# One RWKV step builds its keys in their final tile first and multiplies the decays in afterwards

## The chip, the cores and the metric

One Trainium2 chip, one NeuronCore. The metric is the device time of one execution in microseconds. Below, PE is TensorE, DVE is VectorE, ACT is ScalarE, POOL is GpSimd and SP is the engine that issues most transfers.

## What is computed

The reference is a two-layer backbone. In each layer one input projection feeds a Conformer convolution branch and a bidirectional RWKV-7 branch side by side; an output projection and a SwiGLU feed-forward part follow. 512 latent tokens and 256 context tokens go through the same weights. The part that matters here prepares, for each direction d, the operands of the recurrence:

```python
decay = jnp.exp(-DECAY_SCALE * jax.nn.sigmoid(decay_b0[d] + jnp.tanh(w_lo) @ decay_up[d]))
a = jax.nn.sigmoid(iclr_b0[d] + a_lo @ iclr_up[d])
k_d = k * (1.0 + (a - 1.0) * k_a)
...
s = (s * w_t[:, :, None, :] + sa[..., None] * b_t[:, :, None, :]     # b_t = kk * a
     + v_t[..., None] * k_t[:, :, None, :])
```

The kernel runs the recurrence in chunks of 64 tokens. Within a chunk the running product P of the decays is folded into the operands: `kk` and `r` are multiplied by P, and the two keys, `k_d` and `kk * a`, are divided by P. Products of these scaled operands (Gram matrices) then replace the token-by-token loop.

## The kernel before

**Stages.** Each layer has a mixing stage (projection, convolution and recurrence woven together) and a feed-forward stage. Mixing is cut into 12 blocks: 4 pairs of heads times 3 groups, each of 4 chunks per direction.

**What a block passes through.** `prep(b)` makes the operands of both directions. `grams(b)` multiplies them on PE (the tile names `KR` and `bk` in its matmuls: `pw<-KR,bk`), DVE masks the products into `G`. `base(b)` inverts small triangles by way of DRAM (`G`, `d0`, `Dt`, `XT`, `dimg`, `Tm`) and `levels` extends the inverses. `tokens(b)` transposes `bk` on PE (`pw<-cst,bk`, L938). `chain(b, s)` is the recurrence itself: a round of small steps PE, ACT, PE, ACT/DVE, PE, DVE (`Z`, `UV`, `S`), where each round needs the state `S` of the one before; POOL computes `Q`, the decayed state.

**What sets the order.** On PE the order is written by hand: a plan with first slots and widths weaves these generators between the matmuls of the projection (`pd<-h,wh` and `pd<-h,wl`), 16 slots to a block. In the pass for block b, `prep(b+2)` starts at slot 2 and ends at slot 6, and `z_part(b+2)`, which holds `grams`, stands from slot 9. On DVE, ACT, POOL and SP a scheduler sets the order by priority and readiness when the program is built. DVE also has the taps of the 31-tap convolution to do (`acc<-z,cw,acc`, about 0.9 us each in the first layer).

**`prep` and its tiles.** For each direction two matmuls with `lr` give the raw decays and the raw rates in one PSUM bank `pz`. The scratch `tmp` has three parts: `lx` (the logarithm of the decays, summed by the scan in L867), `px` (its exponential, P) and `qx` (1/P). The scratch `tw` holds tanh of the raw rates. `tmp`, `tw` and `bk` have one buffer each, so direction 1 can start to write `tmp` only when every reader of direction 0's `tmp` is done, and a block's `bk` can be written only when the block before no longer needs it. Within a direction: ACT does a tanh into `lx`, a tanh into `tw` and a scaling; DVE scans; ACT takes two exponentials; then ACT writes the key's factor `e` over `lx` (L233, `tmp<-tw,der`), which has to wait until the exponentials have read `lx`. DVE multiplies `e` by k (`tmp<-tmp,k`), makes (tw+1)*kk in place (`tw<-tw,kk`), makes the one or two parts of `KR`, and ends with the two products with 1/P into `bk` (`bk<-tmp` and `bk<-tw,tmp`). ACT copies a half of `bk` (`bk<-bk`) into a third place and a column of P into `pc`.

Helpers record many operations under one line: `act` L233, `stt` L236, `tt` L239, `ts` L242, `mm` L245.

Of the kernel before, what the change touches and what calls it, by code (L numbers as in the profile page):

```python
# [14 lines left out]
AF = mybir.ActivationFunctionType  # L15
# [166 lines left out]
def net(ctx: ExitStack, tc: tile.TileContext, I, out):  # L182
# [13 lines left out]
    def nm(s):  # L196
        uid[0] += 1
        return f"{s}_{uid[0]}"
# [29 lines left out]
    def bank(tag="w"):  # L228
        pool = {"d": pd, "w": pw, "c": pc_}[tag]
        return pool.tile([128, 512], F32, tag=tag, name=nm("p" + tag))  # L230

    def act(out, in_, func=AF.Copy, **k):
        return A.activation(out=out, in_=in_, func=func, **k)  # L233

    def stt(out, in0, scalar, in1, op0, op1, **k):
        V.scalar_tensor_tensor(out=out, in0=in0, scalar=scalar, in1=in1, op0=op0, op1=op1, **k)  # L236

    def tt(out, a, b, op):
        return V.tensor_tensor(out=out, in0=a, in1=b, op=op)  # L239
# [4 lines left out]
    def mm(out, lhsT, rhs, start=True, stop=True):  # L244
        PE.matmul(out=out, lhsT=lhsT, rhs=rhs, start=start, stop=stop)  # L245
# [15 lines left out]
    MUL, ADD, SUB = ALU.mult, ALU.add, ALU.subtract  # L261
# [354 lines left out]
    for l in range(DEPTH):  # L616
# [9 lines left out]
        der = lp.tile([128, 36], F32, tag="der", name=nm("der"))  # L626
# [201 lines left out]
        def nat(d, gi, cc):  # L828
            if d == 0:
                return (8, 0, 4)[gi] + cc  # L830
            return (11, 7, 3)[gi] - cc

        def dcols(ap, d, gi):

            if d == 0:
                c0 = C * nat(0, gi, 0)
                return ap[:, c0:c0 + 256].rearrange("p (c t) -> p c t", t=64)
            c0 = C * nat(1, gi, 3)
            return ap[:, c0:c0 + 256][:, ::-1].rearrange("p (c t) -> p c t", t=64)
# [3 lines left out]
        def prep(b):  # L843
            p, gi = divmod(b, 3)
            P = PS[p]
            emit = not (last and gi == 0)
            wl = u["wl"]
            KR = s2.tile([128, 2, 4, 2, 64], F32, tag="KR", name=nm("KR"), bufs=3)
            bk = s1.tile([128, 2, 4, 3, 64], F32, tag="bk", name=nm("bk"))
            pc = s2.tile([128, 2, 4], F32, tag="pc", name=nm("pc"), bufs=4)  # L850
            fl = lambda q: q.rearrange("p c t -> p (c t)")
            for d in range(2):
                pz = bank()
                lo = C * (nat(0, gi, 0) if d == 0 else nat(1, gi, 3))
                for j in range(2):
                    mm(pz[:, 256 * j:256 * j + 256], P["lr"][:, d, j, :], wl[:, lo:lo + 256])
                tmp = s1.tile([128, 3, 4, 65], F32, tag="tmp", name=nm("tmp"))
                tw = s1.tile([128, 4, 64], F32, tag="tw", name=nm("tw"))
                rv = lambda q: q if d == 0 else q[:, ::-1]

                lx, px, qx = (tmp[:, j] for j in range(3))
                G.memset(lx[:, :, 0:1], 0.0)  # L862
                act(lx[:, :, 1:65], rv(pz[:, 0:256]).rearrange("p (c t) -> p c t", t=64), AF.Tanh, scale=0.5,
                    bias=der[:, 4 * d + p:4 * d + p + 1])
                act(fl(tw), rv(pz[:, 256:512]), AF.Tanh, scale=0.5, bias=der[:, 8 + 4 * d + p:9 + 4 * d + p])
                act(lx[:, :, 1:65], lx[:, :, 1:65], AF.Copy, scale=-DS / 2, bias=-DS / 2)
                V.tensor_tensor_scan(out=fl(lx), data0=fl(one65), data1=fl(lx), initial=0.0, op0=MUL, op1=ADD)  # L867
                act(fl(px), fl(lx), AF.Exp)
                act(fl(qx), fl(lx), AF.Exp, scale=-1.0)

                e = lx[:, :, 0:64]
                act(e, tw, AF.Identity, scale=der[:, 16 + p:17 + p], bias=der[:, 20 + p:21 + p])
                tt(e, e, dcols(P["k"], d, gi), MUL)
                stt(tw, tw, 1.0, dcols(P["kk"], d, gi), ADD, MUL)
                tt(KR[:, d, :, 0, :], dcols(P["kk"], d, gi), px[:, :, 0:64], MUL)
                if emit:
                    tt(KR[:, d, :, 1, :], dcols(u[f"r{p}"], d, gi), px[:, :, 1:65], MUL)
                tt(bk[:, d, :, 0, :], e, qx[:, :, 1:65], MUL)
                stt(bk[:, d, :, 1, :], tw, 0.5, qx[:, :, 1:65], MUL, MUL)
                act(bk[64:128, d, :, 2, :], bk[64:128, d, :, 0, :])  # L880
                act(pc[:, d, :], px[:, :, 64])
                yield

            vr = s1.tile([128, 4, 64], F32, tag="vr", name=nm("vr"))
            act(vr, dcols(u[f"v{p}"], 1, gi))
            BS[b] = dict(KR=KR, bk=bk, vr=vr, pc=pc, emit=emit, G={}, tT={}, UV={}, T={})
            yield
# [347 lines left out]
        def nsteps(names):  # L1235

            return [-(-c // PCOL) for c in np.cumsum([work(n) for n in names])]
# [29 lines left out]
        with tc.manual_schedule(engines={mybir.EngineType.PE}):  # L1267
            for name, ps in zip(FIRST, pf):
                finish(name, ps)
            e = nsteps(FILL0[l])  # L1270
            B8 = 24 * T / PCOL
            start = {"pair_prep": (pair_prep(0), 3), "prep0": (prep(0), 3), "z0": (z_part(0), 3), "tok00": (tokens(0, 0), 2),
                     "tok01": (tokens(0, 1), 2), "prep1": (prep(1), 3), "z1": (z_part(1), 3), "t0": (t_part(0, 0), 4),
                     "tok10": (tokens(1, 0), 2)}
            weave(*((e[0] + d * B8, w * B8, *reversed(start[n])) for n, (d, w) in plan["prologue"].items()), (0, e[-1], e[-1], proj))
# [5 lines left out]
            for b in range(12):  # L1281
                p, gi = divmod(b, 3)
# [29 lines left out]
                if b + 2 < 12:  # L1312
                    lane("prep", prep(b + 2), 3)
                    lane("z", z_part(b + 2), 3)
                    lane("tok0", tokens(b + 2, 0), 2)
# [176 lines left out]
```

## Time and profile before

| what | value |
|---|---|
| median of 3 runs | 2211.42 us (2211.22 to 2214.58) |
| the profiled execution | 2219.2 us, its span 2217.3 us |
| first layer's mixing stage | about 68 to 620 us of the span |
| second layer's mixing stage | about 1340 to 1800 us |
| PE, DVE, ACT busy over the span | 2064.7, 1451.0, 945.2 us |
| mean granted PE clock | 0.97 of full speed |

Of the profiled execution's 2219.2 us, 1.9 us lie around its span. It was 7.8 us above the median of the runs that were not profiled. All rows of the profile come from this one execution. In a timeline row the first number is the start in microseconds, the second the time to the end of the last of the merged instructions; square brackets give the engine's idle time just before and what ended it.

### The profile page before, as it was taken

Reading aid. Unit: us, or ns where it says so; the run is one execution under the profiler, and the core shown is the slowest. Engines: PE = TensorE matmul, PEld = TensorE weight load, DVE = VectorE, ACT = ScalarE, POOL = GpSimd, SP = SyncE. Lnnn points to the kernel's source line nnn. Section 1 sums busy time; section 2 is a strip of 40 time slices with the busy share of each in tenths; the row PEclk is TensorE's granted clock in tenths of the full one; section 3 lists DMA queues with packets and bytes.
Section 4 is the critical chain, followed back from the end, with each engine's and each line's share of the span. In section 5 each row is a group of like instructions: output and inputs, shape, how many; then the busy total and the mean of one; then the engine's idle time right before and its main releaser. Section 6 shows DMA issues by size and latency. Waiting matters only on the chain.

```text
span 2217.3 us, 44128 instructions
## 1 busy us (share of the span) xinstructions
PE 2064.7 (93%) x17578; PEld 1663.5 (75%) x17578; DVE 1451.0 (65%) x3286; ACT 945.2 (43%) x2186; POOL 203.1 (9%) x528
## 2 busy tenths in 40 slices
PE   5999999998899999999999999999999889999997
PEld 4777777776687888878888876667676568888886
DVE  5578888877758565565653766777877765433446
ACT  4454645555425211212112545665657444222223
POOL 0102131211010000000000000122212010000000
PEclk9999999999899999999999999998999999999998
DMA  7232232243552343343432412121213442333233
GB/s 289 68 82 64 79 85 77 61 109 106 160 192 75 125 142 122 113 146 114 125 113 87 141 41 76 32 62 37 76 35 92 131 148 77 95 98 102 86 98 121
DMA packets 197804, 226.32 MB, mean 102 GB/s; under 512 B 110560, under 2 KB 140000, under 8 KB 197472
## 3 DMA queue, kind: packets, MB, share of 16 engines
q1 hardware_dynamic: 196448, 221.42, 33.2%
q8 instruction: 138, 2.26, 0.4%
q10 hardware_dynamic: 1152, 2.10, 0.2%
q14 instruction: 66, 0.54, 0.1%
HBM read 196.62 MB, written 26.85 MB: 101 GB/s over the span
## 4 chain that ended last, share of the span: by engine, by line
PE 61%; DVE 13%; ACT 10%; issue 7%; DMA 6%; POOL 3%; SPq 0%; POOLq 0%; DVEq 0%; ACTq 0%
PE pd L245 30%; PE pw L245 24%; PE pc L245 5%; DMA at<-in_adaT 4%; ACT tmp L233 2%; DVE wl L239 2%; DVE junk L236 2%; ACT UV L233 1%; DVE acc L236 1%; PE pw L950 1%; PE pw L419 1%; DVE xtmp L239 1%; DVE acc L239 1%; PE pw L938 1%; POOL rq L406 1%
## 5 line engine op out<-in xcount | busy, mean ns | idle before, releaser
L245 PE MATMUL pd<-h,wh 128*128 128x512 f32 (+3 forms) x2496 | 687.3, 365 | 3.6 <-ACT h L233 3.0
L233 ACT ACTIVATE wh<-raw 128x1024 fp32r<-128x1024 f32 (+2 forms) x234 | 220.8, 943 | 675.0 <-PE pw L245 258.7
L245 PEld LDWEIGHTS pd<-h,wh 128*128 128x128 f32 (+1 forms) x2496 | 425.2, 190 | 74.9 <-ACT h L233 3.7
L245 PE MATMUL pd<-h,wl 128*128 128x512 f32 (+3 forms) x1248 | 426.4, 364 | 2.8 <-DVE wl L239 2.8
L239 DVE TENSOR_TENSOR wl<-raw,wh 128x1024 fp32r<-128x1024 f32 (+2 forms) x234 | 253.8, 1085 | 131.4 <-ACT wh L233 130.4
L245 PE MATMUL pw<-h,wh 128*128 128x512 f32 (+1 forms) x1264 | 317.4, 350 | 4.5 <-DVE x L236 2.9
L245 PEld LDWEIGHTS pd<-h,wl 128*128 128x128 f32 (+1 forms) x1248 | 224.1, 190 | 38.7 <-DVE wl L239 4.2
L245 PEld LDWEIGHTS pw<-h,wh 128*128 128x128 f32 x1264 | 211.2, 190 | 40.1 <-DVE x L236 4.8
L236 DVE SCALAR_TENSOR_TENSOR junk<-at,cr 128x1024 bf16<-128x1024 f32 x112 | 136.9, 1223 | 114.2 <-DMA at<-in_adaT 113.2
L236 DVE SCALAR_TENSOR_TENSOR acc<-z,cw,acc 128x497 f32<-128x497 f32 (+20 forms) x216 | 192.9, 893 | 4.3 <-ACT acc L233 2.8
L245 PE MATMUL pw<-h,wl 128*128 128x512 f32 (+1 forms) x632 | 193.0, 351 | 0.0
L245 PE MATMUL pd<-mid,wh 128*128 128x512 f32 (+1 forms) x568 | 139.4, 348 | 10.3 <-ACT mid L233 4.0
L245 PE MATMUL pw<-mid,wh 128*128 128x512 f32 (+1 forms) x568 | 140.0, 350 | 1.1 <-ACT wh L233 1.1
L245 PEld LDWEIGHTS pw<-h,wl 128*128 128x128 f32 x632 | 107.2, 189 | 15.5
L245 PEld LDWEIGHTS pd<-mid,wh 128*128 128x128 f32 x568 | 94.8, 191 | 26.9 <-ACT mid L233 4.6
L245 PEld LDWEIGHTS pw<-mid,wh 128*128 128x128 f32 x568 | 96.7, 195 | 15.0 <-ACT wh L233 1.3
L1058 POOL TENSOR_TENSOR Q<-S,pc 128x128 f32<-128x128 f32 x80 | 53.9, 674 | 527.3 <-DVE S L236 204.2
L239 DVE TENSOR_TENSOR ft<-ft,pw 128x512 f32<-128x512 f32 (+1 forms) x67 | 37.7, 589 | 92.6 <-PE pw L245 92.2
L245 PE MATMUL pd<-mid,wl 128*128 128x512 f32 (+1 forms) x284 | 88.6, 351 | 2.6 <-DVE wl L239 2.4
L245 PE MATMUL pw<-mid,wl 128*128 128x512 f32 (+1 forms) x284 | 88.6, 351 | 0.2 <-DVE wl L239 0.2
L862 POOL MEMSET tmp<- 128x4 f32 x48 | 5.2, 109 | 889.9 <-PE pw L245 638.2
L245 PE MATMUL pw<-KR,bk 64*128 64x128 f32 (+1 forms) x768 | 68.2, 300 | 13.8 <-DVE bk L236 9.0
(208 smaller groups left out, 3177.8 us busy)
## 6 DMA issues: line engine op xcount, KB each, us to landing
raw<-in_wgu SPq DMA_DIRECT2D x88, 512.0 KB, 3.5
at<-in_adaT SPq DMA_DIRECT2D x56, 512.0 KB, 3.7
raw<-in_win SPq DMA_DIRECT2D x42, 512.0 KB, 3.4
ada<-in_ada SPq DMA_DIRECT2D x40, 512.0 KB, 4.5
raw<-in_wd SPq DMA_DIRECT2D x48, 320.0 KB, 2.9
Tm<-dimg SPq DMA_DIRECT2D x96, 128.0 KB, 2.9
raw<-in_wd SPq DMA_DIRECT2D x32, 384.0 KB, 3.0
d<-G SPq DMA_DIRECT2D x96, 64.0 KB, 2.1
```

What stands on the lines that cost most here:

```text
L233: return A.activation(out=out, in_=in_, func=func, **k)
L236: V.scalar_tensor_tensor(out=out, in0=in0, scalar=scalar, in1=in1, op0=op0, op1=op1, **k)
L239: return V.tensor_tensor(out=out, in0=a, in1=b, op=op)
L245: PE.matmul(out=out, lhsT=lhsT, rhs=rhs, start=start, stop=stop)
L406: E.tensor_tensor(out=q, in0=y, in1=y, op=MUL)
L419: PE.transpose(pt[:, c - c0:c - c0 + 128], wide[:, c:c + 128], ident)
L862: G.memset(lx[:, :, 0:1], 0.0)
L938: PE.transpose(pt[hh][:, o:o + 64], bk[hs, d, cc, hh:hh + 2, :].rearrange("p j t -> p (j t)"), ident[hs, hs])
L950: PE.transpose(pv[0:64, o:o + 128], src, ident)
L1058: G.tensor_tensor(out=Q, in0=S, in1=pc[:, :, s:s + 1].to_broadcast([128, 2, 64]), op=MUL)
```

## The change

The factor `e` and both keys are now built in `bk` itself. ACT writes `e` straight to its place in `bk` (b0), DVE multiplies it there by k, and (tw+1)*kk goes to the second place in `bk` (b1) and no longer over `tw`. None of these three steps touches `tmp`, so none of them has to wait for the scan or for the exponentials. Last, both places are multiplied by 1/P in place. The tanh of the rates and the write of `e` are recorded behind the scan and ahead of the exponentials. The number of instructions, and the elements that each handles, are the same.

```diff
                 lx, px, qx = (tmp[:, j] for j in range(3))
+                b0, b1 = bk[:, d, :, 0, :], bk[:, d, :, 1, :]
                 G.memset(lx[:, :, 0:1], 0.0)
                 act(lx[:, :, 1:65], rv(pz[:, 0:256]).rearrange("p (c t) -> p c t", t=64), AF.Tanh, scale=0.5,
                     bias=der[:, 4 * d + p:4 * d + p + 1])
-                act(fl(tw), rv(pz[:, 256:512]), AF.Tanh, scale=0.5, bias=der[:, 8 + 4 * d + p:9 + 4 * d + p])
                 act(lx[:, :, 1:65], lx[:, :, 1:65], AF.Copy, scale=-DS / 2, bias=-DS / 2)
                 V.tensor_tensor_scan(out=fl(lx), data0=fl(one65), data1=fl(lx), initial=0.0, op0=MUL, op1=ADD)
+                act(fl(tw), rv(pz[:, 256:512]), AF.Tanh, scale=0.5, bias=der[:, 8 + 4 * d + p:9 + 4 * d + p])
+                act(b0, tw, AF.Identity, scale=der[:, 16 + p:17 + p], bias=der[:, 20 + p:21 + p])
                 act(fl(px), fl(lx), AF.Exp)
                 act(fl(qx), fl(lx), AF.Exp, scale=-1.0)

-                e = lx[:, :, 0:64]
-                act(e, tw, AF.Identity, scale=der[:, 16 + p:17 + p], bias=der[:, 20 + p:21 + p])
-                tt(e, e, dcols(P["k"], d, gi), MUL)
-                stt(tw, tw, 1.0, dcols(P["kk"], d, gi), ADD, MUL)
+                tt(b0, b0, dcols(P["k"], d, gi), MUL)
+                stt(b1, tw, 1.0, dcols(P["kk"], d, gi), ADD, MUL)
                 tt(KR[:, d, :, 0, :], dcols(P["kk"], d, gi), px[:, :, 0:64], MUL)
                 if emit:
                     tt(KR[:, d, :, 1, :], dcols(u[f"r{p}"], d, gi), px[:, :, 1:65], MUL)
-                tt(bk[:, d, :, 0, :], e, qx[:, :, 1:65], MUL)
-                stt(bk[:, d, :, 1, :], tw, 0.5, qx[:, :, 1:65], MUL, MUL)
+                tt(b0, b0, qx[:, :, 1:65], MUL)
+                stt(b1, b1, 0.5, qx[:, :, 1:65], MUL, MUL)
                 act(bk[64:128, d, :, 2, :], bk[64:128, d, :, 0, :])
                 act(pc[:, d, :], px[:, :, 64])
```

The order on PE is the same, instruction for instruction. On DVE, ACT, POOL and SP the scheduler sets a new one. In the rows below a name's number is that of its buffer, and L867 is the scan.

DVE, direction 1 of the prep whose Gram matmuls stand near 206 us in the first layer, before. `S_2324` is a state of the recurrence, `wl_2343` a weight's low part, `acc_1578` a tap.

```order
L236 SCALAR_TENSOR_TENSOR S_2324<-pc_2319,pc_1135,Q_2264 128x64 x2
L239 TENSOR_TENSOR wl_2343<-raw_2339,wh_2341 128x1024
L867 SCALAR_TENSOR_TENSOR tmp_2246<-one_95,tmp_2246 128x260
L236 SCALAR_TENSOR_TENSOR acc_1578<-z_1299,cw_152,acc_1578 128x775
L239 TENSOR_TENSOR KR_2174<-kk_1787,tmp_2246 128x4x64
L239 TENSOR_TENSOR KR_2174<-r_925,tmp_2246 128x4x64
L239 TENSOR_TENSOR tmp_2246<-tmp_2246,k_1058 128x4x64
L236 SCALAR_TENSOR_TENSOR tw_2247<-tw_2247,kk_1787 128x256
L239 TENSOR_TENSOR bk_2175<-tmp_2246 128x4x64
L236 SCALAR_TENSOR_TENSOR bk_2175<-tw_2247,tmp_2246 128x4x64
```

The same place on DVE in the changed kernel:

```order
L867 SCALAR_TENSOR_TENSOR tmp_2246<-one_95,tmp_2246 128x260
L236 SCALAR_TENSOR_TENSOR bk_2175<-tw_2247,kk_1787 128x4x64
L236 SCALAR_TENSOR_TENSOR S_2324<-pc_2319,pc_1135,Q_2264 128x64 x2
L239 TENSOR_TENSOR bk_2175<-bk_2175,k_1058 128x4x64
L239 TENSOR_TENSOR KR_2174<-kk_1787,tmp_2246 128x4x64
L239 TENSOR_TENSOR KR_2174<-r_925,tmp_2246 128x4x64
L239 TENSOR_TENSOR bk_2175<-bk_2175,tmp_2246 128x4x64
L236 SCALAR_TENSOR_TENSOR bk_2175<-bk_2175,tmp_2246 128x4x64
```

The product with kk and the one with k now stand ahead of the two `KR` rows, two `bk` rows follow these instead of four, the scan and one product have gone ahead of the state, and the weight and the tap have gone behind.

ACT, from direction 0's copy of `bk` to direction 1's exponentials in that prep, before. `wh_2341` is a weight's high part, `XT_1867` belongs to `base`, `UV_1540<-S_2324` carries the state to the next round, `y` and `Z` belong to the recurrence as well.

```order
L233 ACTIVATE wh_2341<-raw_2339 128x1024
L233 ACTIVATE XT_1867<-XT_1867 64x256
L233 ACTIVATE bk_2175<-bk_2175 64x4x64
L233 ACTIVATE tmp_2246<-pw_2243,der_147 128x4x64
L233 ACTIVATE tw_2247<-pw_2243,der_147 128x256
L233 ACTIVATE tmp_2246<-tmp_2246 128x4x64
L233 ACTIVATE UV_1540<-S_2324 64x2x64 x2
L233 ACTIVATE y_1557<-pc_2285 128x64 x2
L233 ACTIVATE Z_2356<-pc_2351 128x128
L233 ACTIVATE tmp_2246<-tmp_2246 128x260 x2
L233 ACTIVATE pc_2176<-tmp_2246 128x4
L233 ACTIVATE tmp_2246<-tw_2247,der_147 128x4x64
```

The same place on ACT in the changed kernel, where direction 0's copy of `bk` stands two rows ahead of the first row:

```order
L233 ACTIVATE tmp_2246<-pw_2243,der_147 128x4x64
L233 ACTIVATE tw_2247<-pw_2243,der_147 128x256
L233 ACTIVATE tmp_2246<-tmp_2246 128x4x64
L233 ACTIVATE bk_2175<-tw_2247,der_147 128x4x64
L233 ACTIVATE XT_1867<-XT_1867 64x256
L233 ACTIVATE tmp_2246<-tmp_2246 128x260 x2
L233 ACTIVATE pc_2176<-tmp_2246 128x4
L233 ACTIVATE y_1557<-pc_2285 128x64
L233 ACTIVATE UV_1540<-S_2324 64x2x64 x2
L233 ACTIVATE y_1557<-pc_2285 128x64
L233 ACTIVATE wh_2341<-raw_2339 128x1024
```

The factor `e` is now written into `bk` ahead of the exponentials, the weight has gone from ahead of direction 1 to behind it, and the state's copy `UV_1540<-S_2324` from ahead of the exponentials to behind them.

DVE again, direction 1 of the prep whose Gram matmuls stand near 1379 us in the second layer, before, from the state on:

```order
L236 SCALAR_TENSOR_TENSOR S_14574<-pc_14569,pc_13754,Q_14549 128x64 x2
L867 SCALAR_TENSOR_TENSOR tmp_14531<-one_95,tmp_14531 128x260
L236 SCALAR_TENSOR_TENSOR acc_14591<-z_14170,cw_13435,acc_14591 128x497
L239 TENSOR_TENSOR KR_14480<-kk_13667,tmp_14531 128x4x64
L242 TENSOR_SCALAR UV_14019<-pc_14597 64x2x64
L239 TENSOR_TENSOR KR_14480<-r_13661,tmp_14531 128x4x64
L239 TENSOR_TENSOR tmp_14531<-tmp_14531,k_13646 128x4x64
L236 SCALAR_TENSOR_TENSOR tw_14532<-tw_14532,kk_13667 128x256
L239 TENSOR_TENSOR bk_14481<-tmp_14531 128x4x64
L236 SCALAR_TENSOR_TENSOR bk_14481<-tw_14532,tmp_14531 128x4x64
```

And in the changed kernel:

```order
L236 SCALAR_TENSOR_TENSOR bk_14481<-tw_14532,kk_13667 128x4x64
L236 SCALAR_TENSOR_TENSOR S_14574<-pc_14569,pc_13754,Q_14549 128x64 x2
L867 SCALAR_TENSOR_TENSOR tmp_14531<-one_95,tmp_14531 128x260
L239 TENSOR_TENSOR bk_14481<-bk_14481,k_13646 128x4x64
L239 TENSOR_TENSOR KR_14480<-kk_13667,tmp_14531 128x4x64
L239 TENSOR_TENSOR KR_14480<-r_13661,tmp_14531 128x4x64
L239 TENSOR_TENSOR bk_14481<-bk_14481,tmp_14531 128x4x64
L236 SCALAR_TENSOR_TENSOR bk_14481<-bk_14481,tmp_14531 128x4x64
L242 TENSOR_SCALAR UV_14019<-pc_14597 64x2x64
```

Here one product stands ahead of the state, the tap has gone behind the prep, and so has the recurrence's `UV_14019`.

## The prediction

> **What bounds the kernel now.** I read the page first, then the busy times by stage, then the waits of PE in the two mixing stages, and last the timeline of single blocks. From the page, the span, PE's share, and the chain that ended last by engine:
>
> ```profile
> span 2217.3 us, 44128 instructions
> PE 2064.7 (93%) x17578; PEld 1663.5 (75%) x17578; DVE 1451.0 (65%) x3286; ACT 945.2 (43%) x2186; POOL 203.1 (9%) x528
> PE 61%; DVE 13%; ACT 10%; issue 7%; DMA 6%; POOL 3%; SPq 0%; POOLq 0%; DVEq 0%; ACTq 0%
> ```
>
> The two mixing stages (length, then PE, PEld, DVE, ACT and POOL busy, then the granted clock):
>
> ```profile
> 68.00:620.00 552.00, 509.06 (x6258) 395.84 (x6257) 437.69 (x1138) 301.99 (x835) 99.42 (x246) 0.96 0.32 88
> 1340.00:1800.00 460.00, 419.91 (x5063) 301.03 (x5061) 331.80 (x956) 273.76 (x772) 87.12 (x223) 0.96 0.28 74
> ```
>
> PE is the bound there too, but it stands idle for 552.00 - 509.06 = 42.9 us and 460.00 - 419.91 = 40.1 us. The change touches these stages alone, and PE's order is unchanged, so it can only win idle time, or clock, of PE. What PE waits for (microseconds in total, times, longest), first layer and then second:
>
> ```profile
> PE pc L245 <- ACT UV L233: 9.2, 9, 1.6
> PE pw L245 <- DVE Tm L1018: 6.4, 10, 1.9
> PE pw L245 <- DVE bk L236: 5.3, 5, 1.7
> PE pw L245 <- ACT bk L233: 2.4, 5, 1.0
> ...
> PE pw L245 <- DMA Tm<-dimg: 7.7, 1, 7.7
> PE pc L245 <- ACT UV L233: 4.2, 8, 0.9
> PE pw L245 <- DVE bk L236: 3.6, 3, 2.1
> PE pw L245 <- ACT bk L233: 0.6, 2, 0.5
> ```
>
> The waits on `bk` are Gram matmuls that stand still until `prep` is done: 5.3 + 2.4 + 3.6 + 0.6 = 11.9 us in 15 waits, a seventh of the idle time. The rest belongs to the recurrence (`UV`), the inverses (`Tm`) and others.
>
> **What a direction of prep costs, and what the change takes off.** The end of one prep in the first layer: the last product of direction 0, then direction 1.
>
> ```profile
> 198.74 0.41 DVE L236 SCALAR_TENSOR_TENSOR bk<-tw,tmp 128x256 f32<-128x256 f32 x1
> 199.08 1.06 ACT L233 ACTIVATE wh<-raw 128x1024 fp32r<-128x1024 f32 x1 [0.62 <-PE pd L245]
> 201.13 0.47 ACT L233 ACTIVATE tmp<-pw,der 128x256 f32<-128x256 f32 x1
> 202.30 0.64 ACT L233 ACTIVATE UV<-S 64x128 f32<-64x128 f32 x2
> 203.78 0.73 ACT L233 ACTIVATE tmp<-tmp 128x260 f32<-128x260 f32 x2
> 204.54 0.60 ACT L233 ACTIVATE tmp<-tw,der 128x256 f32<-128x256 f32 x1
> 204.57 0.42 DVE L239 TENSOR_TENSOR KR<-r,tmp 128x256 f32<-128x256 f32 x1
> 205.18 0.43 DVE L239 TENSOR_TENSOR tmp<-tmp,k 128x256 f32<-128x256 f32 x1 [0.18 <-ACT tmp L233]
> 205.52 0.42 DVE L236 SCALAR_TENSOR_TENSOR tw<-tw,kk 128x256 f32<-128x256 f32 x1
> 205.85 0.42 DVE L239 TENSOR_TENSOR bk<-tmp 128x256 f32<-128x256 f32 x1
> 206.19 0.42 DVE L236 SCALAR_TENSOR_TENSOR bk<-tw,tmp 128x256 f32<-128x256 f32 x1
> 206.66 1.04 PE L245 MATMUL pw<-KR,bk 64*128 64x128 f32 x12 [1.67 <-DVE bk L236]
> ```
>
> On DVE one product starts 0.34 us after the other. Behind the second `KR` product it waits for `e` (0.18 us idle at 205.18, as `e` ends at 205.14), and does two products before the first into `bk`. With `e` and both of these already done, that first product starts at 204.57 + 0.34 = 204.91 in place of 205.85: 0.94 us off the tail. In the second layer:
>
> ```profile
> 1371.03 0.42 DVE L239 TENSOR_TENSOR KR<-r,tmp 128x256 f32<-128x256 f32 x1
> 1371.88 0.43 DVE L239 TENSOR_TENSOR tmp<-tmp,k 128x256 f32<-128x256 f32 x1 [0.43 <-ACT tmp L233]
> 1372.55 0.42 DVE L239 TENSOR_TENSOR bk<-tmp 128x256 f32<-128x256 f32 x1
> 1373.59 0.47 ACT L233 ACTIVATE tmp<-pw,der 128x256 f32<-128x256 f32 x1 [0.17 <-DVE bk L236]
> 1379.33 0.79 PE L245 MATMUL pw<-KR,bk 64*128 64x128 f32 x2 [2.13 <-DVE bk L236]
> ```
>
> Here the same step is 1372.55 - (1371.03 + 0.34) = 1.18 us. The row at 1373.59 shows why both directions count: direction 1's tanh waited on the last product of direction 0, the last reader of `tmp`. So I take 0.94 + 1.18 = 2.1 us per block, about one each for the scratch that is free sooner and for direction 1's own tail. Where another instruction held direction 1 (201.13: ACT was at a weight from 199.08), the new order has that weight behind it, which is worth as much again.
>
> Term 1. A shift of 2.1 us covers every one of the 15 waits but the worst: 2.13 us at 1379.33 and a short one on ACT's copy right behind it. I leave 0.4 us and take 11.5 of the 11.9 us. Bounds: 0, if each wait is replaced by another, and 11.9.
>
> Term 2, the clock. The four rows are a stretch behind a Gram wait each (the columns as above, granted clock third from the end); then the same 16 Gram matmuls at full and at low clock:
>
> ```profile
> 164.00:168.00 4.00, 3.17 (x38) 2.66 (x38) 3.96 (x8) 1.52 (x3) 0.11 (x1) 1.00 0.00 0
> 208.00:212.00 4.00, 4.00 (x32) 2.92 (x26) 3.95 (x6) 0.27 (x1) 0.00 (x0) 0.57 0.38 94
> 283.00:291.00 8.00, 7.19 (x57) 5.79 (x59) 4.57 (x8) 1.00 (x3) 4.39 (x11) 0.57 0.54 148
> 1379.00:1387.00 8.00, 7.67 (x46) 6.03 (x47) 5.68 (x11) 1.61 (x4) 0.87 (x2) 0.57 0.09 18
> ```
>
> ```profile
> 126.17 1.16 PE L245 MATMUL pw<-KR,bk 64*128 64x128 f32 x16
> 210.05 2.03 PE L245 MATMUL pw<-KR,bk 64*128 64x128 f32 x16
> ```
>
> After three of these waits the clock was 0.57, which costs 0.43 x (4.00 + 7.19 + 7.67) = 8.1 us of PE's busy time; after the one at 164 it stayed at 1.00. Without the waits the cause of these stretches would be gone, but low clock follows other idle times too, and one saved here can fall elsewhere. I take half, 4 us; bounds 0 and 8.1.
>
> [...]
>
> Term 3, what is late next. PE arrives sooner at the recurrence, whose waits (9.2 us in 9, 4.2 in 8) are already as long as those on `bk`. If a third of the 15 saved waits lead to one more such wait of 9.2 / 9 = 1.0 us, 5 us come back. Bounds 0 and 11.5.
>
> **Edits that I cost at nothing.** The product and ACT's write into `bk` in place of `tmp` or `tw` keep their length: DVE's rows take 0.42 us into `bk` and into `tw` alike. ACT's `e` into `bk`'s stride has no row; its nearest are 0.60 us into `tmp`, and I keep that. The queue holds the same number of instructions. `bk` is written some 3 us earlier, and it has one buffer; its readers of the block before are out of the way by PE's own order:
>
> ```profile
> 188.27 0.46 PE L938 MATMUL pw<-cst,bk 64*128 64x64 f32 x8
> 190.66 1.13 PE L245 MATMUL pw<-wl,lr 128*128 128x256 f32 x4
> ```
>
> The last transposes of the old `bk` start 2.4 us ahead of the matmuls with `lr` from which the new `bk` comes, so the new wait is 0. On POOL the memset of `tmp` waits for the scratch as before, only less long; what stands behind it is at worst as late as now. On SP one load of the output projection goes back past some twenty transfers, to just ahead of the last block's `Tm`:
>
> ```profile
> 522.93 5.66 SPq L330 DMA_DIRECT2D raw<-in_wo  x2
> 577.47 0.85 ACT L233 ACTIVATE wh<-raw 128x768 fp32r<-128x768 f32 x1
> ```
>
> The second of this pair was used 49 us after it was issued; that distance hides the move. If it did not, PE would wait a few us once. DVE's taps go behind the prep; their reader is blocks away.
>
> **The sum.** 11.5 + 4 - 5 = 10.5 us. The profiled execution would go from 2219.2 to 2208.7 us; the median of the runs stands 7.8 us lower, and I take the same 10.5 us off it: 2211.4 - 10.5 = 2201 us.
>
> **Rivals.**
> - *The clock is not gained*: low stretches fall elsewhere, or never hung on these waits: 11.5 - 5 = 6.5 us, 2205 us. For it: the stretch at 164; against it the three others. 0.17. [...]
> - *Nothing comes back and all of the clock does*: 11.5 + 8.1 = 19.6 us, 2192 us. For it: DVE's idle time on `e` goes too, and in the DVE rows shown a tap or weight moves behind the prep. 0.16.
> - *The next wait takes it all*, or direction 1 is held by other work on ACT, so that the scratch is free sooner for nobody: 0 to 3 us, 2210 us. For it: the row at 201.13. 0.17.
> - *The recurrence is pushed back on ACT: slower.* The copy `UV<-S` (202.30) stood ahead of direction 1's exponentials and stands behind `e` and them in the order shown, 0.60 + 0.73 = 1.3 us. If direction 1 starts 1.3 us sooner nothing is lost; if it is held by its own matmuls, PE waits 1.3 us longer for `UV`. From 11.5 / 1.3 = 9 blocks of the 24 on, this eats term 1; in 14 blocks it gives 18.2 - 11.5 = 6.7 us more, 2218 us. Against it: in the second layer's DVE rows the state goes behind a single product. 0.12.
>
> **How the numbers follow.** My forecast, 2201 us give or take 3, has 0.38. Two of the rivals end faster as well: 0.38 + 0.17 + 0.16 = 0.71 for faster by over 0.2% (4.4 us, about what a measurement of this kernel can tell from no change), 0.17 for within it, 0.12 for slower. The range is 2189 us (all bounds in my favour, 20 us, and 2 more from DVE's idle time) to 2212 us (no gain); outside lie the slower case and a little of the best one.
>
> **What would show it.** Right: PE's waits on `bk` fall from 11.9 to below 2 us; in each direction only two products follow the `KR` products; direction 1's tanh starts about 1 us nearer to direction 0's exponentials; fewer low-clock stretches right behind the Gram matmuls. Wrong: waits of PE on `UV`, `Tm` or `Z` that grow by as much as those on `bk` fall, `UV<-S` later behind `S` than before, or low clock behind other waits for as long as now.

## The result, and the profile after

The changed kernel took 2196.4 us (median) where the kernel before took 2213.0 us beside it: a ratio of 0.991 (95% interval 0.9894 to 0.9927), 17 us less. A second comparison, later and with more runs, gave 2191.8 against 2216.7 us, 0.9887 (0.9873 to 0.9902). The two profiled executions stand 22.3 us apart (spans of 2217.3 and 2195.0 us); how much of that is the kernel's is the first question of the experiments. The page of the changed kernel, for the three lines shown of before:

```profile
span 2195.0 us, 44148 instructions
PE 2049.4 (93%) x17578; PEld 1654.8 (75%) x17578; DVE 1446.8 (66%) x3286; ACT 946.6 (43%) x2186; POOL 216.7 (10%) x528
PE 61%; DVE 13%; ACT 10%; issue 7%; DMA 5%; POOL 2%; SPq 0%; POOLq 0%; DVEq 0%; ACTq 0%
```

Every engine has as many counted instructions as before; the 20 more in the first line are not among these. PE's matmuls are the same 17578, but its busy time is 15.3 us shorter (2064.7 before): between these two executions, most of what the span lost is not idle time but matmuls that ran faster. What PE waits for, in the same two windows of waits as before, first layer and then second (total, times, longest, in us):

```profile
PE pw L245 <- DVE Tm L1018: 9.6, 12, 3.1
PE pc L245 <- ACT UV L233: 7.9, 12, 1.6
PE pw L245 <- DVE k L239: 3.4, 1, 3.4
...
PE pw L245 <- DMA Tm<-dimg: 8.0, 1, 8.0
PE pc L245 <- ACT UV L233: 6.3, 11, 0.9
```

and what its matmuls that read `bk` waited for over the whole kernel:

```profile
  ACT Tm L233: 4.7, 5
  DVE bo L239: 1.4, 2
  DVE G L239: 1.1, 2
  ACT W L233: 0.5, 1
  ACT bk L233: 0.2, 1
```

The waits of the Gram matmuls on `bk`, 11.9 us in 15 before, are one of 0.2 us. `Tm` grew (6.4 to 9.6 in the first layer), `UV` fell there (9.2 to 7.9) and grew in the second (4.2 to 6.3), and a wait on `k` in the first layer grew from 0.7 to 3.4 us. The end of the prep shown of the first layer, its direction 1:

```profile
198.58 0.64 ACT L233 ACTIVATE UV<-S 64x128 f32<-64x128 f32 x2
199.01 0.41 DVE L239 TENSOR_TENSOR KR<-r,tmp 128x256 f32<-128x256 f32 x1
199.34 0.41 DVE L239 TENSOR_TENSOR bk<-bk,tmp 128x256 f32<-128x256 f32 x1
199.35 1.06 ACT L233 ACTIVATE wh<-raw 128x1024 fp32r<-128x1024 f32 x1
199.68 0.41 DVE L236 SCALAR_TENSOR_TENSOR bk<-bk,tmp 128x256 f32<-128x256 f32 x1
200.78 1.16 PE L245 MATMUL pw<-KR,bk 64*128 64x128 f32 x16
```

Only two products follow the `KR` product, the first 0.33 us behind it where it had been 1.28 us (204.57 to 205.85). The weight `wh` runs behind the exponentials, and the 16 Gram matmuls start without a wait. Over all 24 blocks, from the first matmul with `lr` of a block to the end of ACT's second copy into `bk`, prep took 14.68 us on average before and 12.80 us after: 1.9 us less. Direction 0 takes 5.03 us from its tanh to the start of its copy (6.09 before); direction 1's tanh starts 0.74 us after that in both kernels, and from there to the end of its own copy direction 1 takes 5.47 us (6.25 before).

### The profile page after: what moved, and what is told of

Its sections match the earlier page's. It is cut to its first block, busy times and chain, and to the rows that moved or that the text cites. A ratio compares the mean times of both kernels' runs of the same rounds, so it can differ in the third digit from the quotient of the medians.

```text
span 2195.0 us, 44148 instructions
## 1 busy us (share of the span) xinstructions
PE 2049.4 (93%) x17578; PEld 1654.8 (75%) x17578; DVE 1446.8 (66%) x3286; ACT 946.6 (43%) x2186; POOL 216.7 (10%) x528
## 4 chain that ended last, share of the span: by engine, by line
PE 61%; DVE 13%; ACT 10%; issue 7%; DMA 5%; POOL 2%; SPq 0%; POOLq 0%; DVEq 0%; ACTq 0%
PE pd L245 30%; PE pw L245 24%; PE pc L245 5%; DMA at<-in_adaT 5%; DVE wl L239 2%; DVE junk L236 2%; ACT UV L233 2%; ACT tmp L233 2%; DVE acc L236 1%; PE pw L950 1%; ACT bk L233 1%; ACT W L233 1%; PE pw L419 1%; ACT G L233 1%; PE pw L938 1%
## 5 line engine op out<-in xcount | busy, mean ns | idle before, releaser
L1058 POOL TENSOR_TENSOR Q<-S,pc 128x128 f32<-128x128 f32 x80 | 71.0, 888 | 538.7 <-DVE S L236 220.2
L239 DVE TENSOR_TENSOR xtmp<-XT,Dt 64x15 f32<-64x15 f32 (+4 forms) x360 | 73.4, 204 | 10.3 <-DMA Dt<-d 6.2
```

The costliest lines, as they stand in the source:

```text
L1058: G.tensor_tensor(out=Q, in0=S, in1=pc[:, :, s:s + 1].to_broadcast([128, 2, 64]), op=MUL)
```

## The experiments

Each experiment is the kernel before or the changed kernel with the edit shown. In the table *prep* is the time just defined; the waits of PE are those in the two mixing stages; *idle* is PE's idle time, and *low clock* the PE busy time that a granted clock below full cost (the sum of busy time times one less the granted clock, over slices of 1 us). Both are taken from the first to the last matmul with `lr` of a layer, both layers together; *elsewhere* is the low clock's cost in the rest of the span. Each row is one profiled execution; the ratio, from the timed runs, is to the kernel before.

| kernel | prep | bk | UV | Tm | idle | low clock | elsewhere | ratio (95%) |
|---|---|---|---|---|---|---|---|---|
| before | 14.68 | 11.9 | 18.6 | 13.3 | 52.0 | 28.1 | 28.0 | |
| before_again | 14.68 | 12.2 | 19.0 | 13.1 | 53.7 | 18.4 | 26.5 | 0.9995 (0.9982 to 1.0009) |
| after | 12.80 | 0.2 | 20.5 | 15.1 | 44.3 | 14.9 | 30.9 | 0.991 (0.9894 to 0.9927) |
| after_again | 12.78 | 0.2 | 20.2 | 15.2 | 44.9 | 7.8 | 25.1 | 0.9887 (0.9873 to 0.9902) |
| key_only | 13.09 | 0.4 | 20.7 | 14.5 | 45.7 | 13.4 | 36.9 | 0.9945 (0.9924 to 0.9966) |
| gate_only | 14.42 | 8.2 | 19.1 | 12.5 | 50.9 | 18.2 | 38.2 | 0.9991 (0.9975 to 1.0006) |
| late_e | 12.77 | 0.2 | 20.0 | 15.3 | 45.4 | 8.5 | 32.3 | 0.991 (0.9892 to 0.9928) |
| split | 12.59 | 0.2 | 22.3 | 15.7 | 45.6 | 12.7 | 30.0 | 0.9923 (0.9909 to 0.9937) |
| longer_by_one | 13.63 | 3.6 | 20.6 | 11.4 | 46.6 | 13.5 | 41.2 | 0.9943 (0.9924 to 0.9961) |
| longer | 16.00 | 25.2 | 23.3 | 13.1 | 68.1 | 45.1 | 28.6 | 1.0209 (1.0195 to 1.0224) |
| before_z_late | 14.63 | 5.2 | 21.5 | 13.1 | 45.5 | 18.2 | 35.9 | 0.998 (0.9967 to 0.9993) |
| before_early | 15.36 | 3.5 | 35.0 | 10.7 | 64.3 | 23.8 | 29.3 | 1.0062 (1.0048 to 1.0076) |
| after_late | 11.93 | 8.9 | 14.8 | 9.9 | 43.7 | 24.8 | 34.4 | 0.995 (0.9934 to 0.9966) |
| both_late | 11.95 | 1.6 | 12.8 | 11.8 | 40.0 | 24.2 | 41.0 | 0.9957 (0.9941 to 0.9973) |

### What belongs to the kernel and what to the execution

> The kernel before, unchanged, for a second profile of it. What is asked is how much of the difference between the two profiles (22 us of span, of which some 15 us are PE busy time lost to low granted clock in the two mixing stages: 39.5 us before, 24.4 us after) belongs to the kernels and how much to the single execution. Theory 1 (the clock loss belongs to the kernel: it follows the waits on bk): this profile again shows 35 to 42 us of it in the mixing stages, and 11 to 13 us of PE's waits on bk. Theory 2 (much of it is the execution's own chance): 20 to 33 us, with the same waits. The time itself must come out the same, ratio 0.998 to 1.002.

> The changed kernel, unchanged, for a second profile of it and a second comparison of its time. Theory 1 (PE's idle time is the kernel's, the low clock partly the execution's): idle time of PE in the two mixing stages within 2 us of the first profile's, PE busy time lost to low clock within 8 us of it either way; ratio to the kernel before 0.990 to 0.994. Rival (the first comparison was a lucky one): 0.994 to 0.998.

The idle time repeats: 52.0 and 53.7 us before, 44.3 and 44.9 after. The low clock does not: 28.1 and 18.4 us before, 14.9 and 7.8 after. The second profile of before (18.4) went against theory 1, which expected 35 to 42 us (counted in slightly wider windows; 27.5 there), and fits theory 2. `after_again` came out as its theory 1 had it, but for a ratio just below the range. One place shows what varies. The same Gram wait in the second execution of before, and then the time from the wait's end and the 3.40 us behind that, for the first execution (first pair of rows) and the second (granted clock third from the end):

```profile
206.49 1.04 PE L245 MATMUL pw<-KR,bk 64*128 64x128 f32 x12 [1.68 <-DVE bk L236]
```

```profile
206.66:208.50 1.84, 1.84 (x29) 1.65 (x30) 1.80 (x2) 0.19 (x2) 0.11 (x1) 1.00 0.71 197
208.50:211.90 3.40, 3.40 (x20) 2.48 (x19) 3.37 (x6) 0.14 (x1) 0.00 (x0) 0.50 0.34 80
```

```profile
206.49:208.33 1.84, 1.84 (x29) 1.65 (x30) 1.80 (x2) 0.19 (x2) 0.11 (x1) 1.00 0.72 185
208.33:211.73 3.40, 3.40 (x40) 2.60 (x39) 3.37 (x7) 0.47 (x3) 0.00 (x0) 1.00 0.37 88
```

The wait is 1.67 us in the one and 1.68 us in the other, with the same work behind it. In the one PE ran at 0.50 for 3.40 us, beginning 1.84 us after the wait, and ran 20 matmuls; in the other it stayed at 1.00 and ran 40. The traces show most of what goes with it. In each of the 14 profiles, all stretches of low clock begin and end on one grid of 3.413 us that runs through the whole execution: in the two stages of the first of before they begin, among others, at 82.20, 208.49 and 1379.26 us, the last two 37 and 380 steps behind the first, and they last from 3.41 us, one step, to 17.07 us, five steps (1505.56 to 1522.62 us). Low clock goes with how long PE was busy in the window of this grid that has just ended. These are the windows that hold the wait, first execution and then second:

```profile
205.08:208.49 3.41, 1.83 (x29) 1.64 (x30) 3.28 (x6) 0.60 (x3) 0.54 (x3) 1.00 0.63 199
205.27:208.68 3.41, 2.19 (x31) 1.92 (x32) 3.38 (x7) 0.69 (x2) 0.23 (x2) 1.00 0.66 193
```

In the one the wait lies almost wholly in the window, and PE is busy for 1.83 us of it (54%); in the other the grid lies later against the work, and it is 2.19 us (64%). Of all windows at full clock in the two stages of the 14 profiles, 31 had PE busy for less than half, and 29 of these were followed by low clock; at 50 to 60% it was 14 of 34, at 60 to 80% 19 of 316. So in these traces low clock behind a wait goes with how much of the wait falls into one window, and that differs from execution to execution (1.83 and 2.19 us of PE busy in the two above): one profile of each kernel can't size this term.

By the two of each, the change saved 8.2 us of idle time and 11.9 us of low clock in the two stages. The low stretches whose window just ahead holds a wait on `bk` cost 8.4 us in the one execution of before and 5.0 us in the other, and there are none in either of the changed kernel. So 6.7 of the 11.9 us can be laid to those waits; the other 5.2 us belong to stretches behind other waits or matmuls, which both kernels have. The timed runs are a wider sample: the granted clock was 0.9716 on average over 78 runs of before and 0.9756 over the 8 of the changed kernel. On a span of 2195 us that is some 9 us, an estimate.

### The parts of the change

`key_only` keeps `tw` as before; `gate_only` keeps `e` in the scratch; `late_e` writes both keys in `bk` but records the steps in the old order.

```
# key_only, against the changed kernel
-stt(b1, tw, 1.0, dcols(P["kk"], d, gi), ADD, MUL)
+stt(tw, tw, 1.0, dcols(P["kk"], d, gi), ADD, MUL)
-stt(b1, b1, 0.5, qx[:, :, 1:65], MUL, MUL)
+stt(bk[:, d, :, 1, :], tw, 0.5, qx[:, :, 1:65], MUL, MUL)
# gate_only, against the kernel before
-stt(tw, tw, 1.0, dcols(P["kk"], d, gi), ADD, MUL)
+stt(bk[:, d, :, 1, :], tw, 1.0, dcols(P["kk"], d, gi), ADD, MUL)
-stt(bk[:, d, :, 1, :], tw, 0.5, qx[:, :, 1:65], MUL, MUL)
+stt(bk[:, d, :, 1, :], bk[:, d, :, 1, :], 0.5, qx[:, :, 1:65], MUL, MUL)
# late_e, against the changed kernel: two lines moved
+act(fl(tw), rv(pz[:, 256:512]), AF.Tanh, ...)    # ahead of the Copy again
+act(b0, tw, AF.Identity, ...)                    # behind the exponentials again
```

> Half of the change: the first key (e times k) is begun in its final place ahead of the exponentials; the second stays as before (the product with kk back into tw, behind the KR products' scratch as before, then one product into bk). Theory 1 (what counts is how long each direction's chain is): e and its product are off the tail, some 0.6 of the 0.9 us per direction; ratio to the kernel before 0.992 to 0.996, PE's waits on bk 1 to 6 us. Rival (tw must be free too): 0.997 to 1.001.

> The other half alone: e stays in the scratch of the decays behind the exponentials, only the second key's product with kk is written to bk. The chain behind the exponentials keeps e, its product with k and the product with qx. Theory 1 (length of the chain): little is gained, 0.997 to 1.001, PE's waits on bk 9 to 13 us. Rival (that tw is free sooner for the other direction's tanh is what pays): 0.991 to 0.995.

> The third part of the change, the order in which the steps are written: as in the changed kernel both keys are built in bk, but tanh of tw is written ahead of the scale and e behind the exponentials, as in the kernel before. Theory 1 (the order on ACT follows from what waits for what; e runs ahead of the exponentials since its target is no longer the scratch that they read, wherever it is written): ratio to the kernel before 0.987 to 0.993, waits on bk under 1 us, prep ends within 0.2 us of the changed kernel's 12.8. Rival (the written order matters): e ends up behind the exponentials, prep ends 0.4 us or more later, ratio 0.993 to 0.997.

The first key is the change: it alone shortens prep by 1.59 of the 1.88 us and takes the waits on `bk` to 0.4 us. Its ratio, 0.9945, is in the upper part of what theory 1 expected, although its idle time (45.7 us) is nearly that of the changed kernel; its execution lost more to low clock elsewhere (36.9 us). The waits on `bk` are below the 1 to 6 us expected. The second key alone gives 0.26 us of prep, takes the waits on `bk` to 8.2 us (9 to 13 expected), and gives no time that can be told from none. That `tw` is free sooner for the other direction is worth nothing by itself. The order in which the steps are written makes no difference (prep 12.77 us, 0.991): `e` runs ahead of the exponentials there too (195.23 us, the exponentials 196.26 us, in the first layer's prep), since its target is no longer the tile that they read.

### Is it the scratch, or the length of the chain?

`split` gives the three parts of `tmp` a release each, in the same memory; `longer` and `longer_by_one` repeat an exponential.

```
# split, against the changed kernel
-tmp = s1.tile([128, 3, 4, 65], F32, tag="tmp", name=nm("tmp"))
-lx, px, qx = (tmp[:, j] for j in range(3))
+lx, px, qx = (s1.tile([128, 4, 65], F32, tag=t, name=nm(t)) for t in ("lx", "px", "qx"))
# longer (three times; longer_by_one: once), against the changed kernel
 act(fl(qx), fl(lx), AF.Exp, scale=-1.0)
+for _ in range(3):
+    act(fl(qx), fl(lx), AF.Exp, scale=-1.0)
```

> The changed kernel with the scratch tmp cut into three tiles lx, px, qx of the same total size, each with its own release: the other direction's tanh, scale and scan may begin once this direction's exponentials have read lx, and need not wait for its last product. It asks whether scratch that is free sooner is worth something by itself. Theory 1 (with PE's waits on bk at 0.2 us nothing is left to win there): 2193 to 2199 us, prep done 1 to 2 us sooner than in the changed kernel. Rival (the two directions overlapping is what pays, for the room it gives on DVE and ACT): 2183 to 2191 us.

> The changed kernel, PE's order as it is, with the second exponential of each direction done four times over into the same place (three more of 0.36 us each, 1.1 us per direction, about what the change takes off). Theory 1 (length of the chain): PE's waits on bk come back to 7 to 14 us, prep ends 1.5 to 2.5 us later, ratio to the kernel before 0.996 to 1.002. Rival (the new order of taps, weights and prep on the engines is what pays, not the length): 0.990 to 0.994.

> The changed kernel with the second exponential of each direction done twice into the same place, one more of 0.36 us per direction in place of the three more of the kernel 'longer'. Theory 1 (PE waits on bk only where prep ends later than PE comes to the Gram matmuls, so the price rises with the number of blocks without slack, and each wait brings low clock with it): prep ends 0.6 to 1.0 us later than in the changed kernel, waits on bk 1 to 5 us, ratio to the kernel before 0.993 to 0.997. Rival (any instruction more in the chain costs its own length in every block, whatever the slack): 24 blocks times 0.73 us is 17 us more than the changed kernel, ratio 0.998 to 1.001.

With `split`, direction 1's tanh comes 0.84 us sooner behind the block's first matmul (6.49 us in place of 7.33), yet prep ends only 0.2 us sooner (1 to 2 expected) and the time is no better than the changed kernel's. So the scratch was free sooner to no purpose: what the change took off is work between a direction's tanh and its last product.

Adding length back shows the price. With 0.73 us more per block in the chain (`longer_by_one`, prep 0.83 us longer) the waits on `bk` are 3.6 us and the ratio 0.9943, as theory 1 had it. With 2.2 us more (`longer`) prep is 3.2 us longer, the waits on `bk` are 25.2 us and the ratio is 1.0209, all above what either theory expected. PE's waits on `bk` there, first layer and second:

```profile
PE pw L245 <- DVE bk L236: 9.9, 8, 3.0
PE pw L245 <- ACT bk L233: 1.9, 4, 0.9
...
PE pw L245 <- DVE bk L236: 11.3, 8, 3.8
PE pw L245 <- ACT bk L233: 2.1, 4, 1.0
```

and its two windows, above those of the second execution of the changed kernel (length, PE busy, and granted clock third from the end):

```profile
82.11:532.60 450.49, 416.27 (x5075) 324.65 (x5073) 350.49 (x951) 271.21 (x769) 84.17 (x192) 0.95 0.29 75
1320.77:1735.90 415.13, 381.22 (x4340) 279.85 (x4339) 293.41 (x859) 266.94 (x758) 68.33 (x188) 0.94 0.23 55
```

```profile
83.32:503.66 420.34, 397.00 (x5073) 310.26 (x5072) 347.74 (x952) 247.92 (x698) 91.44 (x193) 0.99 0.31 80
1285.76:1669.03 383.27, 361.66 (x4340) 265.89 (x4339) 293.24 (x859) 246.57 (x692) 74.24 (x188) 0.99 0.25 60
```

The same matmuls (5075 and 5073, 4340 and 4340) take 19.27 + 19.56 = 38.8 us more of PE's busy time at a granted clock of 0.95 and 0.94 in place of 0.99. Against the mean of the changed kernel's two executions there are 23.5 us more of idle time, about the 25 us of waits on `bk`, and 34 us more of low clock. Not all of the 34 us is the price of those waits: the stretches whose window just ahead holds a wait on `bk` cost 12.2 us, and those behind a wait on `UV` 21.5 us. How much of the latter the added exponentials caused, and how much this one execution drew, is not shown. PE's order is the changed kernel's throughout.

### Is it when `bk` is ready?

Three kernels move whole steps in PE's order by 0.9 of a slot, 1.9 us, and leave prep's own code alone. (Block 9 keeps its place where prep moves.)

```
# before_early (1.1, on the kernel before), after_late (2.9, on the changed kernel)
-lane("prep", prep(b + 2), 3)
+lanes.append((2 if b == 7 else 1.1, 4, 3, prep(b + 2)))
# before_z_late (on the kernel before); both_late has this and prep at 2.9, on the changed kernel
-lane("z", z_part(b + 2), 3)
+lanes.append((9.9, plan["lanes"]["z"][1], 3, z_part(b + 2)))
```

> The kernel before with its old prep, but the whole of prep(b+2) begins 0.9 of a slot earlier in PE's order (some 1.9 us, the amount by which the change ends prep sooner; the block 9 keeps its place, since its v is not ready then). Theory 1 (all that the change does is that bk is ready 1.9 us sooner for the Gram matmuls): the same gain by another way, 2194 to 2202 us, PE's waits on bk under 3 us. Rival (the gain comes from the shorter chain itself, fewer instructions of prep between the recurrence's on DVE and ACT, or from the new places of taps and weights): 2207 to 2214 us although the waits on bk are gone.

> The changed kernel with prep(b+2) begun 0.9 of a slot later in PE's order (some 1.9 us), which takes back what the change wins in time at the Gram matmuls and keeps its shorter chain. Theory 1 (readiness of bk is all): PE's waits on bk come back to 6 to 14 us, the low clock behind them too, and the time goes to 2206 to 2214 us. Rival (the shorter chain or the new order counts, not the moment at which bk is ready): 2193 to 2201 us.

> The kernel before, with the lane of the Gram matmuls begun 0.9 of a slot (some 1.9 us) later in PE's order and nothing else altered: PE does other work first where it stood and waited for bk. Theory 1 (the waits on bk and the low clock behind them are the whole gain): waits on bk under 2 us, ratio to the kernel before 0.991 to 0.995. Rival (what the change wins is room on DVE and ACT; later Gram matmuls only move the wait to the inverses, Tm, and to the recurrence, UV): 0.997 to 1.003, with Tm and UV longer by what bk loses.

> The changed kernel with prep(b+2) and the lane of the Gram matmuls both begun 0.9 of a slot (some 1.9 us) later in PE's order. With prep alone later the waits on UV and Tm together were 24.7 us against the changed kernel's 35.6, and the waits on bk 8.9 against 0.2. Theory 1 (the later prep gets out of the recurrence's way on ACT and DVE, and the later Gram matmuls take the waits on bk away again): waits on bk under 3 us, on UV and Tm under 30, ratio to the kernel before 0.985 to 0.990, better than the changed kernel. Rival (the waits only move on to the next reader, the inverses of the block behind): 0.991 to 0.997.

`before_early` refutes the plain form of my theory. The waits on `bk` went from 12 to 3.5 us, and the kernel became slower, 1.0062. PE's waits in its first layer:

```profile
PE pc L245 <- ACT UV L233: 20.8, 12, 3.7
PE pw L245 <- DVE Tm L1018: 5.9, 6, 2.6
```

The old prep, begun sooner, took ACT from the recurrence: 20.8 us on `UV` where it was 9.2, with single waits of up to 3.7 us. During the longest, which ends at 236.41 us, DVE is done with the state `S` at 233.82 us, and ACT runs direction 0's copy and direction 1's two tanh ahead of the recurrence's copy of it:

```profile
234.74 0.41 ACT L233 ACTIVATE bk<-bk 64x256 f32<-64x256 f32 x1
235.18 0.47 ACT L233 ACTIVATE tmp<-pw,der 128x256 f32<-128x256 f32 x1
235.56 0.47 ACT L233 ACTIVATE tw<-pw,der 128x256 f32<-128x256 f32 x1
236.05 0.64 ACT L233 ACTIVATE UV<-S 64x128 f32<-64x128 f32 x2
```

So readiness of `bk` is not all; it must be had without more of ACT and DVE at the recurrence's expense. The change does that, since it makes the chain shorter.

`after_late` gives back part of the gain, with 8.9 us of waits on `bk`, as theory 1 said, but less than expected (0.995 in place of about 1), while the waits on `UV` and `Tm` fall to 24.7 us (35.6 in the changed kernel) and prep itself is 0.9 us shorter (11.93 us). Its idle time (43.7 us) is no longer than the changed kernel's; what it gave back is clock, 10.2 of the 24.8 us right behind waits on `bk`. `before_z_late` had 5.2 us of waits on `bk` left, not under 2 us. Its idle time (45.5 us) is as low as the changed kernel's, but its low clock, 18.2 + 35.9 = 54.1 us over the whole span, is as high as before (56.1 and 44.9 us; the changed kernel 45.8 and 32.9), and its gain is a fifth of the changed kernel's. The clock of its 11 timed runs, 0.9698 on average, says the same (before 0.9716, changed 0.9756). So fewer waits on `bk` alone are not the whole gain, against theory 1. In its two stages 6.7 of the 18.2 us stand behind a wait on `bk` and 6.8 behind the 2-column matmuls spoken of below; what costs the clock elsewhere is not shown.

`both_late` was meant as a better kernel, and its idle time is indeed the lowest of all, 40.0 us, but it is slower than the changed kernel. It lost 24.2 us to low clock in the two stages and 41.0 us elsewhere, 26 us more together than the mean of the changed kernel's two executions; the timed runs behind its ratio were granted 0.9686 on average (changed 0.9756). The clock fell there where PE hardly stood still:

```profile
1474.00:1478.00 4.00, 3.95 (x38) 2.92 (x38) 2.44 (x5) 2.87 (x10) 3.40 (x10) 1.00 0.10 27
...
1480.00:1484.00 4.00, 3.81 (x51) 3.05 (x50) 3.88 (x7) 1.32 (x4) 3.54 (x8) 0.50 0.33 99
1484.00:1490.00 6.00, 6.00 (x43) 3.77 (x39) 2.57 (x6) 1.02 (x3) 1.92 (x3) 0.52 0.17 21
```

```profile
1476.45 1.50 PE L245 MATMUL pw<-cst,kk 128*128 128x2 f32 x12
1478.31 0.63 PE L419 MATMUL pw<-cst,gsq 128*128 128x128 f32 x4 [0.36 <-POOL gsq L412]
```

The only wait listed in the 15 us up to 1480 is 0.36 us. Ahead of it stand 12 matmuls of 2 columns, 1.50 us in which PE counts as busy. The window of the grid that ends at 1479.56 holds them all; PE is busy for 3.05 of its 3.41 us with them, and for 1.62 us without them. The same holds in the other profiles. Of the 127 windows at full clock in the two stages that were over 80% busy and hold ten or more of these matmuls, 33 were followed by low clock; of the 2649 others over 80%, none. If the 2-column matmuls are counted as idle time, low clock followed 63 of the 66 windows with PE busy for less than half, 32 of 352 up to three quarters, and none of the 2739 above. So in all these traces the clock goes with them as with idle time; no run takes them out to test it alone. Why this kernel and four others lost 36 to 41 us elsewhere, against 25 to 31 for both executions of both kernels, though nearly all of that code is the same, stays open too: each has one profile.

## Why the prediction was right, and where its size was wrong

The forecast was 10.5 us (2201 us); the comparisons gave 17 and 25 us. The measured 2196.4 us is inside the range of 2189 to 2212 us and outside the forecast's own 3 us either way. The direction, and the mechanism of the waits, held; one term was mis-sized.

- **The shift of 2.1 us per block: right.** Prep is 1.9 us shorter, 1.06 us in direction 0 and 0.78 us in direction 1. The half that was read as scratch free sooner is direction 0's shorter chain: its last product, the last reader of `tmp`, comes sooner, and direction 1 follows at the same distance as before. Scratch that is released sooner without a shorter chain (`split`) gains nothing.
- **Term 1, 11.5 us of the waits on `bk`: right.** 11.7 us went.
- **Term 3, 5 us coming back: about right in size, in part by luck.** All of PE's waits listed in the two mixing stages came from 81.2 to 75.5 us, so 6.0 us came back: `UV` 1.9, `Tm` 1.8 and 2.7 on `k`. PE's idle time between the landmarks fell by 8.2 us on two executions each, which makes it 3.5. Term 1 less term 3 was forecast at 6.5. The forecast laid all 5 us on the recurrence, which took 1.9; `Tm` and `k` were not in it.
- **Term 2, 4 us of clock: the step that failed.** Measured: 11.9 us by two executions each (13.2 by the first pair, 10.6 by the second), some 9 us by the clock of the timed runs. The forecast took half of what stood behind the Gram waits, because a saved stretch could fall elsewhere; all of it went, 8.4 us in the one execution and 5.0 in the other. It was read from one execution, whose next has 0 where I counted 1.7 us (208) and 1.7 where I counted 3.1 us (283). And it took all other stretches for unrelated to the change, but those moved as well: before lost 8.4 us in 1505 to 1523 in the one execution, 1.7 in the other. What of this last part is the change's and what is chance stays open.
- **The rivals.** "The clock is not gained" (2205 us) did not happen: the low stretches behind the waits on `bk`, 8.4 and 5.0 us, went with the waits. Low clock does follow some of these: the stretch shown at 208.50, 3.40 us at 0.50, stands behind a wait of 1.67 us; in the other execution the same wait (1.68 us) is followed by a clock of 1.00. "Nothing comes back and all of the clock does" (2192 us) is nearest in time and half right: the stretches behind the Gram waits did all go, but 6 us came back. "The recurrence is pushed back on ACT" cost 1.9 us on `UV`; as a mechanism it is real, and `before_early` shows it at 16 us (35.0 where it was 18.6). "The next wait takes it all" did not happen.
- **The edits costed at nothing: right.** `e` into `bk` takes 0.60 us as into `tmp`, the products 0.41 us, and no wait for the readers of `bk` appears. DVE's idle time ahead of the second key, which now waits for the tanh of `tw`, is new (8.7 us in both stages); with 0.2 us of waits on `bk` left, it costs PE next to nothing. The load of the out-projection's weight lost most of the cover that I named, since its second half is issued at 555.33 us and used 9.3 us later (49 before), but nothing waits for it:

```profile
555.33 0.42 SPq L330 DMA_DIRECT2D raw<-in_wo  x1
564.59 0.84 ACT L233 ACTIVATE wh<-raw 128x768 fp32r<-128x768 f32 x1
```

## What to carry to other kernels

A value that doesn't depend on the slow step can be begun in its final place ahead of it: what helps is that less stands between the slow step and the waiting engine, not that scratch comes free. Where PE is the bound, price a wait of PE at more than its length (here 12 us of waits on `bk` had 5.0 and 8.4 us of low clock right behind them, 25 us had 12.2), and take two profiles of each kernel before you size the clock's part. Moving work earlier in the order is no substitute for making it shorter: it may take the engine from the chain that others wait for (`before_early`: 35.0 us of waits on `UV` where it was 18.6).

## What was unexpected about the hardware

In all 14 traces the granted clock went low on a grid of 3.413 us that runs through the whole execution, to 0.50 for one to five steps in the two stages of the first of before, and it did so behind a wait of only 1.67 us: the window of the grid with that wait had PE busy for 1.83 of 3.41 us. In the other execution of the same program the same wait (1.68 us) was followed by a clock of 1.00; its window had 2.19 us. Over a whole execution this is a swing of 11 us between the two profiles of before (56.1 and 44.9 us of low clock) and of 13 us between the two of the changed kernel (45.8 and 32.9 us). The clock also fell to 0.50 where the longest wait in the 15 us ahead was 0.36 us, behind matmuls of 2 columns. In these traces such matmuls go with low clock as idle time does: 33 of 127 windows over 80% busy with ten or more of them were followed by it, and none of 2649 others.
